# Retention weight sums: signs turned, and most of the sums made by transfers that add to their target

## The chip, the cores and the metric

The kernel runs on one core of one Trainium2 chip. The metric is the device time of one execution in microseconds (us). TensorE (PE) does the matrix products, VectorE (DVE) and ScalarE (ACT) the elementwise work, SyncE (SP) issues most transfers, and GpSimd (POOL) issues a few.

## What is computed

Two layers over 512 latent and 256 context tokens of width 1024: windowed attention with a SwiGLU FFN, then bidirectional retention with a SwiGLU FFN. The change lies in the second layer's token mixer. Cut to what matters:

```
q_x, k_x, v_x, g_x = split(h_x @ w_qkvg)      # 4 heads: q, k 256 wide, v, g 512 wide
k_c, v_c           = split(h_c @ w_qkvg[...]) # context: keys and values only
ox_f = retention_chunked(q_x, k_x, v_x, log_g[0], state_f)         # forward
ox_b = retention_chunked(flip(q_x), flip(k_x), flip(v_x), ...)     # backward
y    = normalise(ox_f + flip(ox_b)) * gn_gain
out  = (silu(g_x) * y) @ w_o
```

## The kernel before, in words

All products are float32 in three passes: each operand t is split into a high part hi = round(t) by a cast on ACT (L164) and a low part lo = t - hi by a subtraction on DVE (L165), and a product is hi·hi + lo·hi + hi·lo. So each weight chunk of 128 x 1024 float32 (512 KB in HBM, array `wst`) is loaded, cast and subtracted before TensorE reads it.

**The quarter scheme.** For the latent tokens the product of the activations with [k q] (and with [v g]) of one head is done on 2 x 2 blocks with seven quarter products in place of eight (a Winograd form of Strassen's scheme). The activations' quarter sums are made once, in `token_sums` (L1225). The weights' quarter sums are made for each of the four heads, from raw chunks, before they are split. With the block names of the code, before the change:

- k and q (one chunk a block): q12 := q22 - q12 (L1411); r11 := q12 + k11 (L1412); r21 := k21 - r11 (L1415); r11 := q22 - r11 (L1416).
- v and g (two chunks a block, i = 0, 1): g12 := g22 - g12 (L1449); v11 := g12 + v11 (L1450); v21 - v11 (L1456; in head 0 by L1465 and L1466 instead: ACT negates v11, then a transfer issued by POOL adds v21 to it); g12 - v11 (L1537), from raw chunks that are loaded a second time.

Each of these is one DVE instruction on 128 x 1024 elements, apart from head 0's L1465 and L1466.

**The order of a head.** Program order in the loop at L1362: k products and context keys; the k and q sums, their splits and products (`product_q`, L1274), which leave in q and k (tiles `qt`, `kt`) by copies (L1425, L1428, L1437) and by additions (L1431, L1434); rotary positions of q (`rope_pair`, L1296); for heads 1 to 3 the other value products (`other_values`); the v and g sums with the splits w2 (of v11 after L1450), w3 (of g12) and w4 (of the v21 sum); rotary positions of k; the value products 2, 3 and "22" (`product_v`, L1285), with copies out of the two banks `Yv` by ACT: L1478 after product 2, L1481 after product 3, L1487 after "22". Tile 0 of "22" (`last_values(0)`), the first scores, and then tile 1 of "22" (`last_values(1)`) follow. Six rounds of scores and accumulation follow (L1495 to L1531). Then come the splits w1 of the fourth sum (L1537) and w22 of g22, the gate products 1 and 4, which are added to `gate` (L1544, L1597), normalisation, gating, and the output projection (L1609 to L1622).

**Buffers.** Raw chunks go to the ring `wraw` (two buffers) or, where `chunk(i, True)` asks for it, to `wx` (four buffers, which the scores also use). Split weights go to four pairs `whi`/`wlo` that rotate: the split that comes four later waits until TensorE has done with its pair. `chunk` issues on SP (L1204), which takes its transfers one after another and stands still while the next one's buffer is in use.

**Order on the engines.** Every engine executes its own instructions strictly in order. That order is fixed when the kernel is compiled, by a list scheduler with a model of how long instructions and transfers take. It takes, of what its model holds to be ready, what comes first in the program. So L1537, which stands behind the scores in the program, executes ahead of and between them. `after(ins, others)` (L91) puts an instruction behind others on its engine.

Of the kernel before, what the change touches and what calls it, by code (L numbers as in the profile page):

```python
# [11 lines left out]
AF = mybir.ActivationFunctionType  # L12
# [18 lines left out]
HALVES = (slice(0, 256), slice(256, 512))  # L31
# [18 lines left out]
def dit_kernel(ctx, tc, xT, cT, crow, small, consts, masks, tabs0, tabs1, jtab, adaQ, adaN, adaT, wst, out):  # L50
    nc = tc.nc
    mult, add, sub = ALU.mult, ALU.add, ALU.subtract
# [9 lines left out]
    def T(pool, cols, tag, bufs, dt=F32):  # L62
        return pool.tile([P, cols], dt, tag=tag, bufs=bufs, name=tag)

    def pj(n=512):
        return T(psJ, 512, "pj", 2)[:, :n]
# [24 lines left out]
    def after(ins, others):  # L91
        for o in others:
            tc.add_manual_dep(ins.ins, o.ins.name, order, reason="table set turn")
# [32 lines left out]
    def w_parts(pool, own=2):  # L126

        bufs = own
        if ring:
            pool, bufs = ring[wsel[0] % len(ring)], 2  # L130
        elif wsel[0] % (2 + own) < 2:
            pool, bufs = rp, 2
        wsel[0] += 1
        return T(pool, 1024, "whi", bufs, F32R), T(pool, 1024, "wlo", bufs, F32R)
# [28 lines left out]
    def split(t, hi, lo, behind=()):  # L163
        after(nc.scalar.copy(hi, t), behind)  # L164
        return nc.vector.tensor_tensor(lo, t, hi, op=sub)  # L165
# [207 lines left out]
    raw = []  # L373
# [289 lines left out]
    for t in range(6):  # L663
        v = T(akv, 256, "v", 6)
# [134 lines left out]
    t1 = cp.tile([P, 8], F32, name="lg_t1")  # L799
    t2 = cp.tile([P, 8], F32, name="lg_t2")  # L800
# [68 lines left out]
    for d4 in range(0, KT, 4):  # L869
# [4 lines left out]
        for d in range(d4, d4 + 4):  # L874
            o = pj(SX)
# [75 lines left out]
    def token_sums():  # L951

        h1, h2 = THIRDS
        for k in range(4):
            t1, t2 = tm[k], tm[k + 4]
            for j in (k, k + 4):
                nc.scalar.activation(tm[j][:, h1], tm[j][:, h1], AF.Identity, bias=mods[0, 0][:, 3, j:j + 1])
            nc.vector.tensor_tensor(t2[:, h2], t1[:, h2], t2[:, h2], op=add)
            nc.vector.tensor_tensor(t1[:, h2], t1[:, h1], t1[:, h2], op=sub)
            nc.vector.tensor_tensor(t1[:, h1], t2[:, h2], t1[:, h1], op=sub)  # L960
            nc.vector.tensor_tensor(park[:, k * 384:(k + 1) * 384], t2[:, h1], t1[:, h1], op=sub)
            for n, t in ((1, t2[:, h2]), (3, t1[:, h2]), (2, t1[:, h1])):
                S[n, k] = parts(quarter())
                split(t, *S[n, k])
# [226 lines left out]
    qp = R.enter_context(tc.tile_pool(name="qp", bufs=1, reuse_waits="tile"))  # L1191
# [3 lines left out]
    h_sum = [(T(hS, 512, "sA", 16, F32R), T(hS, 512, "sA", 16, F32R)) for _ in range(KT)]  # L1195
# [6 lines left out]
    def chunk(i, own=False):  # L1202
        raw = T(qw, 1024, "wx", 4) if own else T(rp, 1024, "wraw", 2)
        nc.sync.dma_start(raw, wst[i])  # L1204
        return raw

    def split_chunk(raw, behind=()):
        w = w_parts(hpool[0])
        last_split[0] = split(raw, *w, behind)
        return w  # L1210

    last_split, rope_end, rope_sum, hm, other_sums = [None], [None], [None], [], []
# [9 lines left out]
            return lambda k: first(4 * (n[1] == "2") + k, int(n[0]) - 1)  # L1222
        return of

    def token_sums(hm, part, sh2, sums, behind=()):  # L1225

        q1, q2 = HALVES
        shift = mods[1, 0][:, part]
        nc.vector.tensor_tensor(sh2[:, 0:4], shift[:, 0:4], shift[:, 4:8], op=add)
        for k in range(4):  # L1230
            t1, t2 = hm[k], hm[k + 4]
            after(nc.vector.scalar_tensor_tensor(t2[:, q2], t1[:, q2], sh2[:, k:k + 1], t2[:, q2], add, add), behind)
            nc.vector.tensor_tensor(t1[:, q2], t1[:, q1], t1[:, q2], op=sub)
            nc.vector.scalar_tensor_tensor(t1[:, q1], t2[:, q2], shift[:, k:k + 1], t1[:, q1], sub, sub)
            mid = split(t1, *sums[2 * k + 1])
            nc.vector.scalar_tensor_tensor(t2[:, q1], t2[:, q1], shift[:, k + 4:k + 5], t1[:, q1], add, sub)
            other_sums.append((t2, *sums[2 * k]))
        return mid

    def other_parts():  # L1240
        while other_sums:
            split(*other_sums.pop(0))
# [21 lines left out]
    def context_norm(behind):  # L1264
        ssq[1] = t_y(1)
        neg_half_rstd(ssq[1], t_sq(SC), ctx_sum[0], D, behind)
        h, last = norm_mod(1, 1, 0, cres)
        h_ctx.extend(h)
        return last
# [4 lines left out]
    def product_q(o, a, w, first):  # L1274

        for k in range(4):
            xhi, xlo = a(k)
            for e in range(2):
                ws = slice(k * 256 + e * P, k * 256 + e * P + P)
                for i, (p, r) in enumerate(((w[0], xhi), (w[1], xhi), (w[0], xlo))):  # L1280
                    ins = nc.tensor.matmul(o[:, e * SC:(e + 1) * SC], p[:, ws], r, start=first and k + e + i == 0,  # L1281
                                           stop=k == 3 and i == 2, skip_group_check=True)
        return ins
# [77 lines left out]
    normed = context_norm([ins])  # L1361
    for hd in range(RH):  # L1362
        bq = chunk_base + 16 * hd
        bv, bg = bq + 4, bq + 8
# [16 lines left out]
        r11, r21 = chunk(bq), chunk(bq + 1)  # L1381
        k11, k21 = split_chunk(r11), split_chunk(r21)
        if hd == 0:
            sums = token_sums(hm, 0, T(qp, 16, "sh2", 1), h_sum, [normed])
            dx, dcx = strips(0, [sums])
        cos1, sin1 = rope_tables()
        Y, X, kc = W4("Y"), W4("X"), W4("X")
        kt, qt = [[T(qa, 512, "gate", 4) for _ in range(2)] for _ in range(2)]
# [19 lines left out]


        q12, q22 = chunk(bq + 2, True), chunk(bq + 3, True)  # L1410
        nc.vector.tensor_tensor(q12, q22, q12, op=sub)  # L1411
        nc.vector.tensor_tensor(r11, q12, r11, op=add)  # L1412
        w2 = split_chunk(r11, () if hd else [sums])
        other_parts()
        nc.vector.tensor_tensor(r21, r21, r11, op=sub)  # L1415
        nc.vector.tensor_tensor(r11, q22, r11, op=sub)  # L1416
        w1 = split_chunk(r11)
        first = [] if hd else [last_split[0]]
        for ins in later:
# [1 line left out]
        w3, w22, w4 = (split_chunk(r, first) for r in (q12, q22, r21))  # L1421
# [6 lines left out]
            nc.scalar.copy(qt[e][:, HALVES[1]], o)  # L1428
        product_q(Y, quarter_of(3), w3, False)
        for e, o in halves(Y):  # L1430
            nc.vector.tensor_tensor(qt[e][:, HALVES[1]], qt[e][:, HALVES[1]], o, op=add)  # L1431
        product_q(Y2, quarter_of(4), w22, False)
        for e, o in halves(Y2):
            nc.vector.tensor_tensor(qt[e][:, HALVES[0]], qt[e][:, HALVES[0]], o, op=add)  # L1434
        product_q(Y, quarter_of("22"), w4, False)
        for e, o in halves(Y):
            nc.scalar.copy(kt[e][:, HALVES[1]], o)  # L1437
# [5 lines left out]
        g12, w2, w4 = [], [], []  # L1443
        v11 = []
        for i in range(2):
            g12.append(chunk(bg + i, True))
            g22 = chunk(bg + 2 + i, True)
            v11.append(chunk(bv + i))
            nc.vector.tensor_tensor(g12[i], g22, g12[i], op=sub)  # L1449
            nc.vector.tensor_tensor(v11[i], g12[i], v11[i], op=add)  # L1450
            w2.append(split_chunk(v11[i]))
        if hd:
            w3 = [split_chunk(g) for g in g12]
            for i in range(2):
                v21 = chunk(bv + 2 + i, True)
                nc.vector.tensor_tensor(v21, v21, v11[i], op=sub)  # L1456
                w4.append(split_chunk(v21))
        else:

            ready, w3, lows = last_split[:], [], []  # L1460
            for g in g12:
                w3.append(split_chunk(g))
                lows += last_split
            for i in range(2):
                nc.scalar.activation(v11[i], v11[i], AF.Identity, scale=-1.0)  # L1465
                nc.gpsimd.dma_start(v11[i], wst[bv + 2 + i], accum_op=add)  # L1466
            qh = rope_pair(qt, cos1, sin1, ready)
            for low in lows:
                after(low, rope_sum)
# [5 lines left out]
        gate = [T(qa, 512, "gate", 4) for _ in range(4)]  # L1475
# [6 lines left out]
        if hd == 0:  # L1482
            w4 = [split_chunk(v, rope_end) for v in v11]
# [49 lines left out]

        w1 = []
        for i in range(2):
            g, v = chunk(bg + i), chunk(bv + i)
            after(nc.vector.tensor_tensor(g, g, v, op=sub), [] if hd else rope_end)  # L1537
            w1.append(split_chunk(g))
        w22 = [split_chunk(chunk(bg + 2 + i)) for i in range(2)]
        Zg = [W4("Z"), W4("Z")]  # L1540
        last = hd == RH - 1
        product_v(Zg, quarter_of(1), w1, True)
        for t in range(2):
            nc.vector.tensor_tensor(gate[2 + t], gate[2 + t], Zg[t], op=add)  # L1544
        product_v(Zg, quarter_of(4), w22, False, (0,))


# [21 lines left out]
        def gated(n):  # L1569
            silu(gate[n], gate[n])  # L1570
            nc.vector.tensor_tensor(gate[n], ov[n], gate[n], op=mult)
# [22 lines left out]
            turned(HALVES[1])  # L1594
        product_v(Zg, quarter_of(4), w22, False, (1,))
        for t in range(2):
            nc.vector.tensor_tensor(gate[t], gate[t], Zg[t], op=add)  # L1597
            gated(t)
        if not last:

# [23 lines left out]
        for i in range(4):  # L1624
            if i < 2:
                raw = w_raw()
# [20 lines left out]
        hm = [T(hM, 512, "hm", 8) for _ in range(KT)]  # L1647
# [45 lines left out]
    sh2 = T(fp, 48, "sh2", 1)  # L1693
# [263 lines left out]
```

## Time and profile before

| | |
|---|---|
| median of 3 runs | 1734.41 us (1733.25 to 1735.33) |
| profiled execution | 1732.25 us |
| its span in the trace | 1730.3 us |
| retention, 876 to 1366 us: TensorE busy | 485.51 of 490.00 us |
| the same: VectorE, ScalarE, GpSimd busy | 377.12, 233.11, 1.75 us |
| granted TensorE clock | 1.00 in the retention stretch, 0.999 over the span |

The span is the time from the first to the last instruction of the profiled execution; that execution took 1.95 us more in all, and was 2.16 us faster than the median. L1537 is line 1537 of the kernel. An instruction with the letter q behind its engine (SPq) is the sequencer's: it waits or issues. The four heads begin at about 876, 1000, 1123 and 1246 us.

### The profile page before, as it was taken

What the parts mean: (1) busy time and instruction counts of PE and PEld (TensorE: products, weight loads), DVE (VectorE), ACT (ScalarE), POOL (GpSimd) and SP (SyncE); (2) the same over time, 40 slices, a digit from 0 to 9 for tenths busy, and PEclk for the clock granted to TensorE, in tenths of its full rate; (3) what the DMA queues carried; (4) which work ended last, traced back from release to release, by engine and by line L of the source; (5) the groups of instructions that cost most, each with busy time, mean ns of one, the idle gap of its engine ahead of it and who ended that gap; (6) DMA issues with size and microseconds to landing.
All of it is one profiled execution on the core that took longest, in us unless ns stands there. A gap on an engine that the chain in (4) does not pass through costs nothing.

```text
span 1730.3 us, 27786 instructions
## 1 busy us (share of the span) xinstructions
PE 1698.0 (98%) x10876; PEld 1513.0 (87%) x10876; DVE 1361.0 (79%) x2436; ACT 871.1 (50%) x1552; POOL 50.5 (3%) x168
## 2 busy tenths in 40 slices
PE   7999999999999999999999999999999999999999
PEld 5788877899999999999988788898897899899998
DVE  6698889798778788787889858858758798877874
ACT  5587779465433334342556534524525464445442
POOL 0000000000000000000000000000000000000000
PEclk9999999999999999999999999999999999999999
DMA  9612221543253434343423524523423223333322
GB/s 349 239 30 57 62 62 56 209 134 121 73 157 117 153 110 148 123 154 102 156 99 88 183 77 132 163 82 124 159 90 108 95 74 103 117 102 116 100 86 86
DMA packets 62803, 207.48 MB, mean 120 GB/s; under 512 B 7248, under 2 KB 8912, under 8 KB 62416
## 3 DMA queue, kind: packets, MB, share of 16 engines
q1 hardware_dynamic: 55184, 178.97, 32.0%
q0 software_dynamic: 7200, 26.22, 5.2%
q8 instruction: 85, 1.39, 0.3%
q10 hardware_dynamic: 288, 0.52, 0.1%
q14 instruction: 46, 0.38, 0.1%
HBM read 199.65 MB, written 2.10 MB: 117 GB/s over the span
## 4 chain that ended last, share of the span: by engine, by line
PE 78%; DVE 11%; DMA 6%; ACT 3%; issue 2%; SPq 0%; ACTq 0%; DVEq 0%
PE Y L897 14%; PE pj L147 7%; PE Z L897 7%; PE pj L149 7%; PE pj L148 7%; PE Z L1292 6%; PE X L897 3%; DMA wraw<-in_wst_dram 3%; PE pT L736 2%; PE pO L750 2%; PE S L710 2%; DVE wlo L165 2%; PE Y L1281 2%; PE pj L1292 2%; PE X L1281 1%
## 5 line engine op out<-in xcount | busy, mean ns | idle before, releaser
L164 ACT CAST whi<-wraw 128x1024 fp32r<-128x1024 f32 x258 | 270.0, 1051 | 333.7 <-PE Z L149 81.9
L165 DVE TENSOR_TENSOR wlo<-wraw,whi 128x1024 fp32r<-128x1024 f32 x258 | 314.3, 1221 | 64.5 <-ACT whi L164 62.7
L897 PE MATMUL Y<-aq,whi 128*128 128x384 f32 x640 | 173.5, 335 | 0.6 <-ACT hn L1053 0.6
L897 PEld LDWEIGHTS Y<-aq,whi 128*128 128x128 f32 x640 | 116.6, 188 | 1.6 <-ACT hn L1053 1.4
L256 DVE SCALAR_TENSOR_TENSOR res<-pj,mod,res 128x512 f32<-128x512 f32 (+1 forms) x112 | 81.0, 728 | 41.5 <-PE pj L149 41.2
L897 PE MATMUL Y<-aq,wlo 128*128 128x384 f32 x320 | 107.0, 334 | 0.0
L273 DVE CUSTOM_DVE_ANT_0 y<-adaw,crow,small_sb 128x1024 bf16<-128x1024 f32 x64 | 81.9, 1280 | 29.6 <-DMA adaw<-in_adaT_dram 29.4
L1292 PE MATMUL Z<-whi,sA 128*128 128x512 f32 x256 | 81.7, 394 | 1.4 <-ACT gate L1478 1.4
L101 ACT ACTIVATE pr<-pr,stat,qs 128x513 f32<-128x513 f32 (+2 forms) x96 | 74.2, 775 | 9.1 <-DVE stat L717 8.8
L147 PE MATMUL pj<-ax,whi 128*128 128x512 f32 x176 | 69.0, 392 | 1.2 <-DVE res L256 1.2
L149 PE MATMUL pj<-ax,whi 128*128 128x512 f32 x176 | 68.6, 390 | 0.0
L148 PE MATMUL pj<-ax,wlo 128*128 128x512 f32 x176 | 68.6, 390 | 0.0
L147 PE MATMUL pj<-act,whi 128*128 128x512 f32 x168 | 65.6, 391 | 0.0
L148 PE MATMUL pj<-act,wlo 128*128 128x512 f32 x168 | 65.5, 390 | 0.0
L149 PE MATMUL pj<-act,whi 128*128 128x512 f32 x168 | 65.5, 391 | 0.0
L897 PEld LDWEIGHTS Y<-aq,wlo 128*128 128x128 f32 x320 | 60.1, 188 | 0.0
L1292 PEld LDWEIGHTS Z<-whi,sA 128*128 128x128 f32 x256 | 48.0, 188 | 13.0 <-ACT gate L1478 2.6
L711 DVE CUSTOM_DVE_ANT_0 pr<-S,mask,qs 128x256 f32<-128x256 f32 (+1 forms) x96 | 53.1, 566 | 7.8 <-PE S L710 5.3
L897 PE MATMUL Y<-sA,whi 128*128 128x256 f32 x304 | 58.1, 277 | 0.6 <-ACT res L1746 0.6
L897 PE MATMUL Y<-hx,whi 128*128 128x256 f32 x304 | 56.3, 277 | 0.0
L736 PE MATMUL pT<-const_sb,pr 128*128 128x128 f32 x352 | 53.6, 278 | 1.5 <-ACT tt L738 0.9
L1292 PE MATMUL Z<-wlo,sA 128*128 128x512 f32 x128 | 50.7, 396 | 0.2
(581 smaller groups left out, 5070.4 us busy)
## 6 DMA issues: line engine op xcount, KB each, us to landing
wraw<-in_wst_dram SPq DMA_DIRECT2D x224, 512.0 KB, 3.6
adaw<-in_adaT_dram POOLq DMA_DIRECT2D x48, 512.0 KB, 3.9
wx<-in_wst_dram SPq DMA_DIRECT2D x30, 512.0 KB, 4.3
adan<-in_adaQ_dram SPq DMA_DIRECT2D x16, 512.0 KB, 8.8
adan<-in_adaN_dram SPq DMA_DIRECT2D x12, 512.0 KB, 7.7
adaw<-in_adaT_dram SPq DMA_DIRECT2D x8, 512.0 KB, 3.9
res<-in_xT_dram SPq DMA_DIRECT2D x14, 256.0 KB, 3.2
aq<-in_adaN_dram SPq DMA_DIRECT2D x12, 256.0 KB, 5.7
```

Of the source, the lines that this page charges most:

```text
L101: ins = nc.scalar.activation(*args, **kw)
L147: nc.tensor.matmul(o, whi, xhi, start=first, stop=False)
L148: nc.tensor.matmul(o, wlo, xhi, start=False, stop=False)
L149: return nc.tensor.matmul(o, whi, xlo, start=False, stop=last)
L164: after(nc.scalar.copy(hi, t), behind)
L165: return nc.vector.tensor_tensor(lo, t, hi, op=sub)
L256: return nc.vector.scalar_tensor_tensor(res[d], o, mods[l, s][:, part, d:d + 1], res[d], mult, add)
L273: res.append(nc.vector.tensor_tensor_reduce(junk, w, cr[:, s * 1024:(s + 1) * 1024], 1.0, sm_t[:, C_ADAB + l * 48 + j:C_ADAB + l * 48 + j ...
L711: nc.vector.tensor_tensor_reduce(pt[:, c0:c0 + w], bank, mask[:, m0:m0 + w], 1.0, top, add, ALU.min, lo)
L736: nc.tensor.transpose(tp[:, a * P:(a + 1) * P], self.pr[(0, 2, 1, 3)[a]][:, ki * P:(ki + 1) * P], ident)
L897: nc.tensor.matmul(o, p, r, start=first and k + i == 0, stop=k == 3 and i == 2, skip_group_check=not first)
L1292: ins = nc.tensor.matmul(os[t], p, r, start=first and k + i == 0, stop=k == 3 and i == 2, skip_group_check=by_k or not first)
```

## The change

It turns the signs so that the sums are plain additions: q12 + q22, g12 + g22, v11 + v21 and g12 + v11 take the place of the differences. The difference of signs is taken up in the activations' quarter sums (two operators of `token_sums` turned for this layer) and in four places where product banks are added to `qt` and `gate`, which become subtractions of the same shape. The four sums named are then no longer made by DVE: a transfer issued by POOL reads the second operand from HBM and adds it to the first, which an earlier transfer has put into SBUF. Head 0's negation on ACT goes. r21 := k21 + r11, r11 := r11 - q22, r11 := q12 + k11 and v11 := g12 + v11 stay on DVE.

The raw chunks g22 (first load), v21 and the second v11 are no longer loaded to a buffer of their own. v11 stays in its `wraw` buffer until v21 has been added and the sum has been split (as in head 0 before). In head 0, L1537 stood behind the rotary work (`rope_end`); nothing takes the place of that order for w1.

```diff
+    def add_chunk(raw, i):
+        nc.gpsimd.dma_start(raw, wst[i], accum_op=add)
...
-    def token_sums(hm, part, sh2, sums, behind=()):
+    def token_sums(hm, part, sh2, sums, behind=(), ops=(add, sub)):
...
-        nc.vector.tensor_tensor(sh2[:, 0:4], shift[:, 0:4], shift[:, 4:8], op=add)
+        plus, minus = ops
+        nc.vector.tensor_tensor(sh2[:, 0:4], shift[:, 0:4], shift[:, 4:8], op=plus)
...
-            after(nc.vector.scalar_tensor_tensor(t2[:, q2], t1[:, q2], sh2[:, k:k + 1], t2[:, q2], add, add), behind)
+            after(nc.vector.scalar_tensor_tensor(t2[:, q2], t1[:, q2], sh2[:, k:k + 1], t2[:, q2], add, plus), behind)
...
-            nc.vector.scalar_tensor_tensor(t2[:, q1], t2[:, q1], shift[:, k + 4:k + 5], t1[:, q1], add, sub)
+            nc.vector.scalar_tensor_tensor(t2[:, q1], t2[:, q1], shift[:, k + 4:k + 5], t1[:, q1], add, minus)
...
-            sums = token_sums(hm, 0, T(qp, 16, "sh2", 1), h_sum, [normed])
+            sums = token_sums(hm, 0, T(qp, 16, "sh2", 1), h_sum, [normed], (sub, add))
...
         q12, q22 = chunk(bq + 2, True), chunk(bq + 3, True)
-        nc.vector.tensor_tensor(q12, q22, q12, op=sub)
+        add_chunk(q12, bq + 3)
         nc.vector.tensor_tensor(r11, q12, r11, op=add)
         w2 = split_chunk(r11, () if hd else [sums])
         other_parts()
-        nc.vector.tensor_tensor(r21, r21, r11, op=sub)
-        nc.vector.tensor_tensor(r11, q22, r11, op=sub)
+        nc.vector.tensor_tensor(r21, r21, r11, op=add)
+        nc.vector.tensor_tensor(r11, r11, q22, op=sub)
...
-            nc.vector.tensor_tensor(qt[e][:, HALVES[1]], qt[e][:, HALVES[1]], o, op=add)
+            nc.vector.tensor_tensor(qt[e][:, HALVES[1]], qt[e][:, HALVES[1]], o, op=sub)
...
-            nc.vector.tensor_tensor(qt[e][:, HALVES[0]], qt[e][:, HALVES[0]], o, op=add)
+            nc.vector.tensor_tensor(qt[e][:, HALVES[0]], o, qt[e][:, HALVES[0]], op=sub)
...
             g12.append(chunk(bg + i, True))
-            g22 = chunk(bg + 2 + i, True)
+            add_chunk(g12[i], bg + 2 + i)
             v11.append(chunk(bv + i))
-            nc.vector.tensor_tensor(g12[i], g22, g12[i], op=sub)
             nc.vector.tensor_tensor(v11[i], g12[i], v11[i], op=add)
             w2.append(split_chunk(v11[i]))
         if hd:
             w3 = [split_chunk(g) for g in g12]
             for i in range(2):
-                v21 = chunk(bv + 2 + i, True)
-                nc.vector.tensor_tensor(v21, v21, v11[i], op=sub)
-                w4.append(split_chunk(v21))
+                add_chunk(v11[i], bv + 2 + i)
+                w4.append(split_chunk(v11[i]))
         else:
...
             for i in range(2):
-                nc.scalar.activation(v11[i], v11[i], AF.Identity, scale=-1.0)
-                nc.gpsimd.dma_start(v11[i], wst[bv + 2 + i], accum_op=add)
+                add_chunk(v11[i], bv + 2 + i)
...
-            g, v = chunk(bg + i), chunk(bv + i)
-            after(nc.vector.tensor_tensor(g, g, v, op=sub), [] if hd else rope_end)
+            g = chunk(bg + i)
+            add_chunk(g, bv + i)
             w1.append(split_chunk(g))
...
-            nc.vector.tensor_tensor(gate[2 + t], gate[2 + t], Zg[t], op=add)
+            nc.vector.tensor_tensor(gate[2 + t], Zg[t], gate[2 + t], op=sub)
...
-            nc.vector.tensor_tensor(gate[t], gate[t], Zg[t], op=add)
+            nc.vector.tensor_tensor(gate[t], Zg[t], gate[t], op=sub)
```

## The prediction, made before the changed kernel ran

> **What bounds the kernel now.** I read the page's busy shares first, then the windows of the four heads, then what TensorE, DVE and SP waited for there.
>
> ```profile
> PE 1698.0 (98%) x10876; PEld 1513.0 (87%) x10876; DVE 1361.0 (79%) x2436; ACT 871.1 (50%) x1552; POOL 50.5 (3%) x168
> ```
> ```profile
> 876.00:1000.00 124.00, 120.83 (x666) 102.91 (x664) 111.23 (x180) 74.57 (x125) 1.75 (x2) 1.00 0.44 136
> 1000.00:1123.00 123.00, 122.89 (x653) 104.69 (x652) 90.18 (x122) 54.62 (x81) 0.00 (x0) 1.00 0.38 119
> 1123.00:1246.00 123.00, 122.81 (x653) 104.69 (x652) 90.03 (x121) 54.51 (x81) 0.00 (x0) 1.00 0.38 121
> sum 490.00, PE 485.51 PEld 413.36 DVE 377.12 ACT 233.11 POOL 1.75; mean PE 121.38 PEld 103.34 DVE 94.28 ACT 58.28 POOL 0.44
> ```
> ```profile
> PE Z L1292 <- ACT gate L1478: 1.4, 1, 1.4
> PE Y L1281 <- DVE wlo L165: 0.8, 1, 0.8
> PE X L1519 <- ACT wx L164: 0.5, 1, 0.5
> PE pj L147 <- ACT qk L1587: 0.5, 1, 0.5
> PE X L1582 <- DVE gate L1571: 0.5, 1, 0.5
> PE Z L1292 <- DVE wlo L165: 0.4, 1, 0.4
> ```
>
> The second fence has, after the stretch, the busy time of PE, weight loads, DVE, ACT and POOL, then the granted clock, the DMA share and GB/s; its last row sums the four heads. TensorE bounds the stretch: 485.51 of 490.00 us busy. DVE, which the change relieves, is busy 111.23 of 124 us in head 0, where TensorE has 3.2 us idle, and about 90 of 123 in heads 1 and 2, where TensorE has 0.11 and 0.19 us idle. So **no relief of DVE can bring more than 4.5 us**. The third fence splits 4.1 us of that; the waits on L1587 and L1571 (1.0 us) are the last head's end, which the change doesn't touch. **3.5 us** are left as the most that can be won, nearly all in head 0.
>
> **What goes from DVE and ACT.** Rows of DVE's groups, then single lines:
>
> ```profile
> L1537 DVE TENSOR_TENSOR wraw<-wraw 128x1024 f32<-128x1024 f32 x8 | 9.8, 1221 | 8.4 <-DMA wraw<-in_wst_dram 8.4
> L1449 DVE TENSOR_TENSOR wx<-wx 128x1024 f32<-128x1024 f32 x8 | 9.8, 1219 | 2.1 <-DMA wx<-in_wst_dram 2.1
> L1456 DVE TENSOR_TENSOR wx<-wx,wraw 128x1024 f32<-128x1024 f32 x6 | 7.1, 1214 | 0.0
> ```
> ```profile
> L1411 DVE TENSOR_TENSOR wx<-wx x4: 1215/1216/1219, 891.1 to 1238.9; 128x1024 f32<-128x1024 f32 x4
> ```
> ```profile
> L1412 DVE TENSOR_TENSOR wraw<-wx,wraw x4: 1209/1224/1225, 915.5 to 1258.1; 128x1024 f32<-128x1024 f32 x4
> ```
> ```profile
> 925.71 0.33 SPq L1204 DMA_DIRECT2D wx<-in_wst_dram  x1
> 927.98 0.33 SPq L1204 DMA_DIRECT2D wraw<-in_wst_dram  x1
> ```
> ```profile
> 930.02 1.22 DVE L1449 TENSOR_TENSOR wx<-wx 128x1024 f32<-128x1024 f32 x1 [0.93 <-DMA wx<-in_wst_dram]
> ...
> 932.96 1.22 DVE L1450 TENSOR_TENSOR wraw<-wx,wraw 128x1024 f32<-128x1024 f32 x1
> ```
> ```profile
> DMA to landing us min/median/max: 3.4/3.7/7.8
> ```
>
> The last row is of the loads that `chunk` issues (L1204). DVE loses 8 + 8 + 6 + 4 = 26 instructions of 1.22 us, 31.7 us in all; ACT loses head 0's two negations. This counts only where TensorE waits. In head 0, L1449 for i = 1 waits for a g22 that SP could issue only at 925.71, since the `wx` buffers were full. Without g22 in `wx` the two q and two g chunks fill its four buffers at the head's start, and L1450 waits only for v11: issued 927.98, plus 3.7, is 931.7, against 932.96. The rotary chain and the copy L1478 behind it come 1.3 us earlier, so 1.3 of the 1.4 us go. The 0.5 us on `wx` lies behind the splits of the late w22 chunks, which come earlier; I take it whole. The 0.8 us (L1281) stands behind L1412 and L1416, which stay. **Gain 1.8 us**; ends 0 and 3.5. Where a sign turns, operation and shape stay: L1411 (a subtraction) 1216 ns, L1412 (an addition) 1224. Cost nothing.
>
> **What the transfers cost.** Only head 0 has had such additions, two of them:
>
> ```profile
> L1466 POOL DMA_DIRECT2D wraw<-in_wst_dram x2: 861/872/884, 934.4 to 939.0; - x2
> ...
> DMA to landing us min/median/max: 5.3/5.7/6.1
> ```
> ```profile
> 934.00:946.00 12.00, 10.64 (x52) 8.61 (x52) 11.49 (x19) 6.99 (x12) 1.75 (x2) 1.00 0.54 87
> 1028.00:1033.00 5.00, 5.00 (x47) 5.00 (x46) 0.97 (x3) 0.65 (x2) 0.00 (x0) 1.00 0.34 105
> 980.00:1000.00 20.00, 20.00 (x98) 16.68 (x96) 18.31 (x31) 12.29 (x18) 0.00 (x0) 1.00 0.61 208
> ```
>
> An addition holds POOL 0.87 us and lands 5.7 us after issue, 4.5 us later than a 1.22 us DVE sum that starts with it; and it starts only when its target has landed. On the DMA engines the two took 0.54 x 12 / 2 = 3.2 us each (nothing else was issued there); one plain load took 0.34 x 5 = 1.7 us. Heads 1 to 3 get seven additions for six loads: 22.4 - 10.2 = 12.2 us of 123, so the share rises from 0.38 to 0.48. POOL gets 6.1 us in a head where it now has 0.00, and issues in the order in which targets land; SP issues six fewer.
>
> *q12 and g12: nothing.* L1411 runs at 891.1 and 1238.9, L1412 after it at 915.5 and 1258.1: the sum lies 24 and 19 us ahead of its reader, cover for 4.5 us. Without it L1412, the split w2 and TensorE would be late by the difference.
>
> *v21: nothing in heads 1 to 3, with little to spare.* Head 1, ACT, then DVE:
>
> ```profile
> 1065.84 1.05 ACT L164 CAST whi<-wx 128x1024 fp32r<-128x1024 f32 x1 [0.63 <-PE Z L1292]
> 1068.18 1.04 ACT L164 CAST whi<-wx 128x1024 fp32r<-128x1024 f32 x1
> ```
> ```profile
> 1060.59 1.21 DVE L1456 TENSOR_TENSOR wx<-wx,wraw 128x1024 f32<-128x1024 f32 x1
> 1061.72 1.21 DVE L165 TENSOR_TENSOR wlo<-wraw,whi 128x1024 fp32r<-128x1024 f32 x1
> ```
>
> The first two are the casts of w4: their `whi` pair is TensorE's until then. The addition to v11[1] can be issued after w2's last subtraction, which ends at 62.93 and moves up by some 1.2 us without L1456; plus 5.7 is 1067.4, ahead of 68.18. Head 0's w4 stands behind the rotary work anyway.
>
> *w1: this costs.* Before, its chunk loads hung only on L1456. Now v11 keeps its `wraw` buffer until w4 is split, and two transfers come in series.
>
> ```profile
> 1073.52 1.06 ACT L164 CAST whi<-wraw 128x1024 fp32r<-128x1024 f32 x1 [1.17 <-DVE wraw L1537]
> 1074.48 0.58 ACT L1481 COPY gate<-Z 128x512 f32<-128x512 f32 x1
> ```
> ```profile
> 1076.73 0.39 PE L1292 MATMUL Z<-whi,aq 128*128 128x512 f32 x1
> ```
> ```profile
> 1079.60 1.22 DVE L1537 TENSOR_TENSOR wraw<-wraw 128x1024 f32<-128x1024 f32 x1 [1.98 <-DMA wraw<-in_wst_dram]
> ```
> ```profile
> 1202.89 1.23 DVE L1537 TENSOR_TENSOR wraw<-wraw 128x1024 f32<-128x1024 f32 x1 [2.00 <-DMA wraw<-in_wst_dram]
> ```
>
> The first cast of w1 (73.52) stands on ACT ahead of the copy L1481, which frees the bank that TensorE needs at 76.73. And the compiled order believes in fast transfers: twice here DVE stands 2 us before L1537 for a chunk that has not landed. With two transfers in series that error grows, and the cast will stand as early as now. Sum: w4[0] cast 1065.84 + 1.05, its subtraction 1.22 = 1068.1; load 3.7 = 1071.8; addition 5.7 = 1077.5; cast 1.06 = 1078.6; copy 0.58 = 1079.2. TensorE is held 2.4 us; **7.3 us in heads 1 to 3**. Behind the cast on ACT also stand L1487 and the scores' casts; on DVE the cast's subtraction stands before the first scores' multiplication. If L1481 comes first, these are what is held, so much the same time is at stake. Ends: nothing (the cast placed after all that TensorE waits for), and 4.1 us a head (subtraction as late as it is now, landing at 6.1 and some sharing), 12.3 in all; I take the sum from the medians. In head 0 two rounds of scores are ready before w1's cast; nothing there.
>
> **Sum.** -1.8 + 7.3 = +5.5 us. The profiled execution took 1732.25 us (span 1730.3, and 1.95 around it), 2.16 under the median; so 1737.8 for it and **1739.9** for a median like that shown.
>
> **Rivals.** *The additions stay hidden* (ends faster): the cast of w1 stands behind L1481 and the first scores' cast, or the addition lands 2.5 us sooner than my sum (1075.0 instead of 1077.5), from which point nothing is held. Then the gain stands alone: 1734.41 - 1.8 = 1732.6, at best 1730.9. For it: TensorE needs w1 itself only at the end of the scores. Against: the rows of L1537. The Trainium skill's "DMA: Bandwidth & Descriptors", section "Anatomy of one DMA — SWDGE (gpsimd) path", gives a transfer that GpSimd issues 2.0 us plus its bytes at 436 GB/s, by my estimate 3.2 us for 512 KB; by that rule w1 would land at 1075.0 and this rival would hold. The trace's 5.3 to 6.1 us for the adding transfers speaks against it.
>
> *Transfers get in each other's way*, on top of the forecast. After a head's scores the DMA share is 0.61 already (980 to 1000); three additions for one load bring 0.61 x 20 + 9.6 - 1.7 = 20.1 us of work into 20.
>
> ```profile
> 992.29 1.06 ACT L164 CAST whi<-wraw 128x1024 fp32r<-128x1024 f32 x1 [1.05 <-DMA wraw<-in_wst_dram]
> 993.25 0.63 ACT L107 ACTIVATE gate<-gate 128x512 f32<-128x512 f32 x1
> ```
> ```profile
> 996.65 0.38 PE L1582 MATMUL X<-const_sb,gate 128*128 128x128 f32 x2
> ```
>
> A weight load behind one addition lands 3.2 us later and holds ACT, with the gate's activation behind it; that ends at 993.9 and has some 2 us before the transposes at 996.65. 1.2 us in each of heads 0 to 2: 1743.5.
>
> *Nothing moves*: other waits take what DVE gives back, and w1 is hidden: 1734.4.
>
> **Chances.** Forecast 0.48 (its own range 1735 to 1743), hidden 0.30, contention 0.12, nothing 0.10. A measurement of this kernel tells about 0.2%, 3.5 us, from no change, so the bounds are 1730.9 and 1737.9. Faster: 0.14 of the hidden case (a little more relief than I count) and 0.01 of the forecast: 0.15. Same: 0.16 + 0.10 + 0.12 of the forecast: 0.38. Slower: 0.35 + 0.12 = 0.47. The range 1731.5 to 1744.5 leaves out the better half of the hidden case's spread and the tail of contention.
>
> **What would show it.** Right: in heads 1 to 3 ACT or DVE stands some 4 us before w1's cast for a transfer, and TensorE waits 2 to 3 us for L1481 or for a cast of the scores; head 0's wait on L1478 is under 0.3 us; L1466's kind lands 5 to 6 us after issue. Wrong: TensorE idle stays under 0.3 us in heads 1 to 3, or w4's casts wait for their addition, or the casts of w1 come after the first scores.

## The result, and the profile after

The kernel after took 1746.72 us (median of 6 runs, 1744.82 to 1750.77) against 1734.20 us for the kernel before beside it (6 runs): **slower by 12.5 us**, ratio 1.0072 with a 95% interval of 1.0061 to 1.0083. The forecast was 1739.9 us, and the range ended at 1744.5. The profiled execution of after took 1750.77 us, with a span of 1748.6 us, so it is the slowest of the six. Line numbers of after lie 1 to 4 above those of before from L1285 on: the scores' matmuls are L1507 to L1509, their accumulation L1520 to L1522, the first scores' multiplication L1512, and the new transfers L1208.

The page's busy line and TensorE's waits in the retention stretch, 876 to 1380 us (waiting instruction, what it waited for, total us, times, longest):

```profile
PE 1708.5 (98%) x10876; PEld 1520.8 (87%) x10876; DVE 1333.2 (76%) x2410; ACT 868.9 (50%) x1550; POOL 72.7 (4%) x194
```
```profile
PE X L1520 <- ACT wx L164: 9.1, 4, 2.8
PE X L1522 <- DVE wx L165: 1.8, 3, 0.6
PE Z L1296 <- DVE wlo L165: 1.1, 2, 0.7
```

DVE is busy 27.8 us less, as meant (31.7 were forecast). Head 0's wait for the copy of `gate` has gone from the list. In its place stands one wait in each of the four heads, for a cast of the scores. TensorE's busy time *rose* by 10.5 us although it executes the same 10876 matmuls; that is a second loss, shown further down.

The timeline of head 1 in after shows where the wait comes from (start, duration, engine, line, in brackets the idle time before it and what ended it):

```profile
1075.39 0.87 POOL L1208 DMA_DIRECT2D wraw<-in_wst_dram  x1 [10.27 <-DMA wraw<-in_wst_dram]
1075.59 0.59 ACT L1482 COPY gate<-Z 128x512 f32<-128x512 f32 x1 [2.16 <-PE Z L1296]
...
1078.08 0.86 POOL L1208 DMA_DIRECT2D wraw<-in_wst_dram  x1 [1.81 <-DMA wraw<-in_wst_dram]
...
1082.22 1.05 ACT L164 CAST whi<-wraw 128x1024 fp32r<-128x1024 f32 x1 [6.04 <-DMA wraw<-in_wst_dram]
...
1083.30 1.23 DVE L165 TENSOR_TENSOR wlo<-wraw,whi 128x1024 fp32r<-128x1024 f32 x1 [10.49 <-ACT whi L164]
1083.39 0.39 PE L1509 MATMUL pj<-qk 128*128 128x512 f32 x1
1084.44 0.68 DVE L1512 SCALAR_TENSOR_TENSOR hn<-pj,dx 128x512 f32<-128x512 f32 x1
...
1084.93 1.04 ACT L164 CAST whi<-wraw 128x1024 fp32r<-128x1024 f32 x1 [1.18 <-DMA wraw<-in_wst_dram]
1085.88 0.61 ACT L164 CAST wx<-hn 128x512 fp32r<-128x512 f32 x1
...
1086.54 0.79 PE L1520 MATMUL X<-wx 128*128 128x512 f32 x1 [2.76 <-ACT wx L164]
```

The two additions of w1 are issued at 1075.39 and 1078.08 and land 6.7 and 6.8 us later. ACT stands 6.04 us before w1's first cast for the first of them. DVE stands 10.49 us before that cast's subtraction, and the first scores' multiplication (L1512) is behind it. ACT stands another 1.18 us for the second addition, and the cast of the first scores (1085.88) is behind that. TensorE, which needs this cast, issues its last matmul at 1083.39 and its next at 1086.54.

**The second loss is the clock.** Stretches of after around that pause (stretch, length, then busy us of PE, weight loads, DVE, ACT and POOL; the third number from the end is the granted clock):

```profile
1078.00:1083.70 5.70, 5.70 (x26) 4.41 (x24) 0.40 (x1) 1.48 (x2) 0.86 (x1) 1.00 0.93 165
1086.50:1089.90 3.40, 3.24 (x7) 2.13 (x8) 3.12 (x5) 2.56 (x4) 0.00 (x0) 0.50 0.69 237
1089.90:1093.30 3.40, 3.40 (x11) 2.64 (x10) 2.50 (x4) 1.67 (x2) 0.00 (x0) 0.56 0.55 159
1093.30:1098.00 4.70, 4.70 (x22) 3.90 (x21) 2.43 (x4) 1.24 (x2) 0.00 (x0) 1.00 0.42 124
...
1215.80:1219.20 3.40, 3.40 (x8) 2.73 (x9) 2.71 (x4) 1.70 (x3) 0.00 (x0) 0.50 0.53 166
...
1342.10:1345.50 3.40, 2.94 (x7) 2.39 (x8) 3.34 (x5) 1.73 (x3) 0.00 (x0) 0.50 0.52 154
...
966.50:969.90 3.40, 2.79 (x7) 2.15 (x7) 3.40 (x6) 1.93 (x3) 0.00 (x0) 0.52 0.55 154
969.90:973.30 3.40, 3.40 (x9) 2.64 (x8) 2.12 (x3) 2.28 (x3) 0.00 (x0) 0.50 0.53 154
```

Before the pause the clock is 1.00, behind it 0.50 to 0.56 for 6.8 us, then 1.00 again. Heads 2 and 3 have 3.4 us of it, head 0 has 6.8. The account of the profiled execution: pauses of 2.19, 2.93, 2.52 and 2.15 us (from the distances of the matmuls' starts, less the usual 0.23) make 9.8 us, and six stretches of 3.4 us at half clock lose 10.2 us, 20.0 together. That agrees with the starts of the same matmuls in before: around the scores the four heads fall back by 5.0, 5.6, 4.6 and 3.9 us, 19.1 in all. Ahead of the scores head 0 gains 2.0 us and heads 1 to 3 gain 1.4, so the retention stretch loses 15.6 us of the 18.3 by which the spans differ. Of the rest, 0.2 us come before this stretch and 2.5 behind it; the record shows no cause for these. The six runs of after differ along with their clock: two with a mean clock of 0.992 took 1750.6 and 1750.8 us, four with 0.994 took 1744.8 to 1746.8. The only trace is of the slowest of them; which falls of the clock the faster four lack is not on record.

### The profile page after: what moved, and what is told of

Its sections match the earlier page's. It is cut to its first block, busy times and chain, and to the rows that moved or that the text cites. A ratio compares the mean times of both kernels' runs of the same rounds, so it can differ in the third digit from the quotient of the medians.

```text
span 1748.6 us, 27807 instructions
## 1 busy us (share of the span) xinstructions
PE 1708.5 (98%) x10876; PEld 1520.8 (87%) x10876; DVE 1333.2 (76%) x2410; ACT 868.9 (50%) x1550; POOL 72.7 (4%) x194
## 4 chain that ended last, share of the span: by engine, by line
PE 77%; DVE 10%; DMA 8%; ACT 3%; issue 2%; SPq 0%; ACTq 0%; POOLq 0%; DVEq 0%
PE Y L897 13%; PE pj L147 7%; PE pj L149 7%; PE pj L148 7%; PE Z L897 6%; DMA wraw<-in_wst_dram 4%; PE Z L1296 4%; PE X L897 3%; PE Y L1285 3%; PE pT L736 2%; DVE wlo L165 2%; PE pj L1296 2%; PE pO L750 2%; PE S L710 2%; PE X L1285 2%
## 5 line engine op out<-in xcount | busy, mean ns | idle before, releaser
L164 ACT CAST whi<-wraw 128x1024 fp32r<-128x1024 f32 x264 | 276.3, 1050 | 346.2 <-PE Z L149 80.2
L165 DVE TENSOR_TENSOR wlo<-wraw,whi 128x1024 fp32r<-128x1024 f32 x264 | 321.8, 1222 | 114.4 <-ACT whi L164 113.3
L1296 PE MATMUL Z<-whi,sA 128*128 128x512 f32 x256 | 80.9, 392 | 0.0
L1296 PEld LDWEIGHTS Z<-whi,sA 128*128 128x128 f32 x256 | 48.0, 188 | 10.3
L1296 PE MATMUL Z<-wlo,sA 128*128 128x512 f32 x128 | 50.4, 394 | 0.7 <-DVE wlo L165 0.7
```

Source lines behind the costliest of these rows:

```text
L1296: ins = nc.tensor.matmul(os[t], p, r, start=first and k + i == 0, stop=k == 3 and i == 2, skip_group_check=by_k or not first)
```

## The experiments

The theory, called W: ACT and DVE stand in their fixed order for w1's late additions, the scores' casts behind them hold TensorE, and each pause also costs clock. The rivals: L, the load that the adding transfers put on the DMA engines; H, which keeps W's pause but lays w1's lateness on v21's addition, which keeps the buffers that w1's loads need; and that the clock does not matter. Every time below is compared with runs of the kernel before on the same chip; the ratio is given with its 95% interval.

| kernel | median us | before beside it | ratio |
|---|---|---|---|
| after | 1746.72 | 1734.20 | 1.0072 (1.0061 to 1.0083) |
| v21_w1_by_dve | 1730.32 | 1734.96 | 0.9974 (0.9963 to 0.9985) |
| only_w1 | 1734.05 | 1734.96 | 0.9996 (0.9987 to 1.0006) |
| w1_by_dve | 1732.75 | 1734.84 | 0.9988 (0.9979 to 0.9998) |
| w1_in_wx | 1736.91 | 1734.25 | 1.0014 (1.0004 to 1.0024) |
| filled_idle | 1740.26 | 1734.96 | 1.0032 (1.0019 to 1.0046) |
| w1_behind_2 | 1739.25 | 1734.96 | 1.0024 (1.0010 to 1.0037) |
| w1_2_out_behind | 1727.51 | 1734.25 | 0.9964 (0.9953 to 0.9976) |
| v21_w1_dve_out_behind | 1729.04 | 1734.25 | 0.9971 (0.9960 to 0.9981) |
| before_out_behind | 1735.39 | 1734.84 | 1.0003 (0.9993 to 1.0012) |
| head0_only | 1732.32 | 1734.25 | 0.9990 (0.9981 to 1.0000) |

### Which sums cost: v21 and w1 given back to DVE

```diff
-                add_chunk(v11[i], bv + 2 + i)
-                w4.append(split_chunk(v11[i]))
+                v21 = chunk(bv + 2 + i, True)
+                nc.vector.tensor_tensor(v21, v21, v11[i], op=add)
+                w4.append(split_chunk(v21))
...
-            g = chunk(bg + i)
-            add_chunk(g, bv + i)
+            g, v = chunk(bg + i), chunk(bv + i)
+            after(nc.vector.tensor_tensor(g, g, v, op=add), [] if hd else rope_end)
```

> The sum of w1 in all heads and that of v21 in heads 1 to 3 are DVE's again, with loads of their own; q12's and g12's sums stay transfers that add. Theory W (ACT stands in its fixed order before w1's cast for a late addition, the scores' cast behind it holds TensorE, and TensorE's clock falls after each such pause): all pauses go and the gain of head 0 stays, 1732.6 us, 1731 to 1735. Rival L (the load that adding transfers put on the DMA engines, whichever sum they make): 12 of the 26 additions stay, so some half of the loss stays, 1738 to 1742.

Measured 1730.32 us, faster than before by 4.6 and 0.7 below W's range. All four pauses ahead of the scores are gone; so W's account of them holds, and the load of the other additions is not the loss. One long pause is new, 2.95 us at head 0's transposes, with 3.4 us at half clock behind it. TensorE's wait and, below it, ACT at that place:

```profile
PE X L1584 <- DVE gate L1573: 3.2, 2, 2.8
```
```profile
993.90 1.04 ACT L164 CAST whi<-wraw 128x1024 fp32r<-128x1024 f32 x1 [5.61 <-DMA wraw<-in_wst_dram]
994.85 0.63 ACT L107 ACTIVATE gate<-gate 128x512 f32<-128x512 f32 x1
```

The cast belongs to the output projection's weights. ACT stands 5.61 us for their load, and the last gate activation stands behind it.

### w1's sum alone by transfer

Here q12, g12 and, in heads 1 to 3, v21 are DVE's sums with loads of their own, and w1 stays as in after.

```diff
-        add_chunk(q12, bq + 3)
+        nc.vector.tensor_tensor(q12, q22, q12, op=add)
...
+            g22 = chunk(bg + 2 + i, True)
-            add_chunk(g12[i], bg + 2 + i)
+            nc.vector.tensor_tensor(g12[i], g22, g12[i], op=add)
...
-                add_chunk(v11[i], bv + 2 + i)
-                w4.append(split_chunk(v11[i]))
+                v21 = chunk(bv + 2 + i, True)
+                nc.vector.tensor_tensor(v21, v21, v11[i], op=add)
+                w4.append(split_chunk(v21))
```

> Only w1's sum is a transfer that adds; q12, g12 and v21 in heads 1 to 3 are DVE sums with loads of their own, as before. Theory W without a part for v21: w1's additions pause TensorE in all four heads, and head 0's gain is missing: 1734 plus 14 to 18, 1748 to 1752 us. Rival H (w1 is late because v21's addition keeps v11 in the wraw buffers that w1's loads need; w1's addition alone would be early enough): pauses in head 0 alone, where v21 was added by a transfer before too: 1734 plus 5, 1738 to 1741. Rival L: 8 additions more than before, 1736 to 1740, with no pause at a place of its own.

Measured 1734.05 us, the same as before: better than any theory had it. POOL, then ACT, in head 1 of this kernel:

```profile
1068.60 0.86 POOL L1208 DMA_DIRECT2D wraw<-in_wst_dram  x1 [108.50 <-ACT wx L164]
1070.86 0.85 POOL L1208 DMA_DIRECT2D wraw<-in_wst_dram  x1 [1.40 <-DVE hn L1305]
```
```profile
1078.71 1.05 ACT L164 CAST whi<-wraw 128x1024 fp32r<-128x1024 f32 x1 [1.27 <-DMA wraw<-in_wst_dram]
...
1081.66 0.62 ACT L164 CAST wx<-hn 128x512 fp32r<-128x512 f32 x1 [1.41 <-DVE hn L1514]
```

w1's additions start at 1068.60 and 1070.86, 6.8 and 7.2 us earlier than in after, since v11 leaves its `wraw` buffer early. Both of w1's casts stand ahead of the scores' cast here too, and yet that one (1081.66) waits only for its own scores. So **in heads 1 to 3 the addition to w1 alone costs nothing**. In head 0, where v21 was added by a transfer before the change too, TensorE pauses: 1.3 us and, two matmuls later, 0.8 us, and one stretch of lowered clock follows. That is some 3 us in place of H's 5, and heads 1 to 3 give it back: the 1860 matmuls whose starts I compare below take 346.8 us in this kernel, 348.6 in before.

### v21's sum alone by transfer, w1's by DVE

The diff is the lower half of the first one.

> The kernel after with w1's sum alone given back to DVE, with loads of its own; v21, q12 and g12 stay transfers. Theory H (v21's addition keeps both wraw buffers, and w1's four loads must go through them one pair after the other): w1 is still late in heads 1 to 3, TensorE pauses 1 to 1.5 us ahead of the second scores, too short for the clock: 1733 to 1737 us. Rival (w1's own addition is all that is late): no pause there, 1729 to 1731, as with v21 on DVE as well.

Measured 1732.75 us. TensorE waits 1.8 us in all (three times, 0.6 at most) ahead of the second scores, about half of what H had; the time lies 0.25 us below its range and above the rival's. So v21's addition alone costs little. Only **both in series** make w1 late enough for a long pause, as after has them in every head and only_w1 in head 0.

### The same transfers, with w1's loads in other buffers

`w1_chunks(own)` is w1's loop of loads, additions and splits, with `chunk(bg + i, own)`:

```diff
+        if hd:
+            w1 = w1_chunks(True)
         pend = scores(0)
...
+        if hd == 0:
+            w1 = w1_chunks(False)
```

> The kernel after, with w1's chunks of heads 1 to 3 in the wx buffers, which come free ahead of v11's wraw, so that they are loaded and added to without waiting for v21; all sums stay transfers, and w1's casts stand as early on ACT as before. Theory H (the hold of v11's buffers makes w1 late): no pause ahead of the scores in heads 1 to 3, head 0's stays; pauses at the transposes as in w1_behind_2 may come: 1732 to 1739. Rival (w1's addition is too slow at that place in any buffer): 1744 to 1749.

Measured 1736.91 us, 9.8 below after. The pauses ahead of the scores in heads 1 to 3 are gone, though every sum is still a transfer: H again. (The edit also moves w1's loop ahead of the scores in the program, so that its transfers are issued earlier; no run separates the place from the buffers.) Shorter waits came ahead of that place, for subtractions of weights and for the copy that frees a bank of `gate`:

```profile
PE Z L1296 <- DVE wlo L165: 3.3, 5, 0.8
PE Z L1296 <- ACT gate L1479: 3.1, 3, 1.1
```

What holds these two was not followed further.

### The idle time filled with matmuls

```diff
         for m in range(1, 6):
             cur = scores(m)
+            if hd and m == 1:
+                for _ in range(8):
+                    nc.tensor.matmul(ov[0], kh[0][0][:, 0:P], qh[0][0], start=True, stop=True)
             accumulate(m - 1, *pend)
```

> The kernel after, with eight extra matmuls of 512 columns (1.8 us at full clock, their sums are overwritten) in heads 1 to 3 at the place where TensorE pauses, so that it stands only 0.3 to 1.1 us there. Theory C (about half of the loss, some 2 us a pause, is the clock that falls to half after a pause): the clock stays up in these heads, 1740 us, 1737 to 1742, though more is computed. Rival (the pause alone is the loss, or the clock falls for another reason): 1746 to 1749.

Measured 1740.26 us: 24 matmuls more, and 6.5 us less than after. TensorE's wait, and stretches behind the place of the pause in heads 1, 2 and 3:

```profile
PE X L1520 <- ACT wx L164: 3.5, 4, 1.4
```
```profile
1086.40:1089.80 3.40, 3.40 (x17) 2.81 (x16) 2.71 (x4) 1.53 (x2) 0.00 (x0) 1.00 0.62 164
1207.80:1211.20 3.40, 2.76 (x11) 1.98 (x12) 3.40 (x5) 2.65 (x4) 0.00 (x0) 1.00 0.54 171
1334.30:1337.70 3.40, 2.79 (x11) 2.02 (x12) 3.40 (x5) 2.59 (x4) 0.00 (x0) 1.00 0.58 171
```

The clock is 1.00 in all three. These matmuls bring the scores no earlier, so it is the idle time that lowers the clock. How much the clock costs is read from the half-clock stretches of after (10.2 us), not from this median: head 0, where nothing was added, had a pause of 0.8 us and no fall in this execution and so lost 4.3 us less than in after's profile. Around their scores heads 1 to 3 fall back by 10.2 us against before, where after has 14.1; those 3.9 us are what the added matmuls brought, their own time included.

### w1's casts put behind the third round's scores

```diff
-            split(sd, ss[:, 0:512], ss[:, 512:])
+            sc_end.append(split(sd, ss[:, 0:512], ss[:, 512:]))
...
-            w1.append(split_chunk(g))
+            w1.append(split_chunk(g, [sc_end[2]]))
```

> All transfers as in the kernel after; w1's two casts are put behind the cast of the third round's scores in ACT's order, so that the first two rounds no longer stand behind them. Theory W: the additions have landed by then, no pause, clock near 1.00, 1732.6 us, 1731 to 1735. Rival L: the same transfers at the same places, 1744 to 1748.

Measured 1739.25 us: neither. The pauses ahead of the scores are gone, and three others stand at the transposes of heads 0 to 2. TensorE's wait, then ACT, SP and the clock at the end of head 1:

```profile
PE X L1584 <- DVE gate L1573: 6.2, 3, 2.5
```
```profile
1113.45 0.63 ACT L107 ACTIVATE gate<-gate 128x512 f32<-128x512 f32 x1 [1.29 <-DVE gate L1599]
1119.67 1.04 ACT L164 CAST whi<-wraw 128x1024 fp32r<-128x1024 f32 x1 [5.58 <-DMA wraw<-in_wst_dram]
1120.62 0.62 ACT L107 ACTIVATE gate<-gate 128x512 f32<-128x512 f32 x1
```
```profile
1111.65 10.68 SPq L122 DMA_DIRECT2D wraw<-in_wst_dram  x3
```
```profile
1119.00:1122.60 3.60, 1.13 (x6) 0.65 (x4) 1.83 (x2) 2.90 (x4) 0.00 (x0) 1.00 0.70 198
1122.60:1126.00 3.40, 3.37 (x16) 3.37 (x17) 1.23 (x1) 2.55 (x4) 0.00 (x0) 0.51 0.48 154
```

A weight load issued at 1111.65, among three additions of the next head's sums, lets its cast begin only at 1119.67, 8 us later, and the last gate activation stands behind it. (Plain loads can crowd each other as well: of five that SP issued in before from 976.60 to 980.74, the last took 7.8 us.) This is the prediction's contention rival at the very place it named, larger than its 1.2 us. In after it does not show: there the casts behind the late load came after the activations.

### And the projection's casts put behind the last gate activation

```diff
-                w.append(next_w(hpool[0]))
+                w.append(next_w(hpool[0], behind=turn["silu"][-1:]))
```

> The kernel w1_behind_2 (all transfers of the kernel after; w1's casts behind those of the third scores) with one more change of order: the casts of the output projection's weights in heads 0 to 2 stand on ACT behind the last gate activation. In w1_behind_2 TensorE paused 1.5, 2.7 and 2.6 us at the transposes, behind a gate activation that stood behind such a cast, whose plain load had landed 8 us after issue among three additions. Theory Q (a late transfer costs only through what stands behind it in a queue): these pauses and the clock behind them go, 1728 to 1731 us. Rival S (the load is late for TensorE itself, which then waits for the projection's weights): 1735 to 1739.

Measured 1727.51 us, below the interval's lower end by 0.5: ratio 0.9964 (0.9953 to 0.9976). **This version beats both kernels, and it makes all the transfers of after.** The profile is of its slowest run, 1731.49 us. TensorE's longest waits in the retention stretch, and ACT at the end of head 1:

```profile
PE pj L147 <- ACT qk L1589: 1.0, 2, 0.6
PE Z L1296 <- DVE wlo L165: 0.8, 2, 0.4
PE X L1521 <- ACT wx L164: 0.6, 1, 0.6
```
```profile
1116.27 0.63 ACT L107 ACTIVATE gate<-gate 128x512 f32<-128x512 f32 x1 [1.70 <-DVE gate L1599]
...
1122.71 1.05 ACT L164 CAST whi<-wraw 128x1024 fp32r<-128x1024 f32 x1 [2.07 <-DMA wraw<-in_wst_dram]
```

ACT still stands 2.07 us for a weight load, with nothing behind it that TensorE needs soon. Theory Q holds: a late transfer costs through what is queued behind it.

### Controls of that order, and of the gain

> The kernel v21_w1_by_dve (1730.3 us; its one long pause, 2.9 us, stood at head 0's transposes behind the same cast) with the casts of the output projection's weights behind the last gate activation. Theory Q: 2.9 us and 1.7 of clock go, 1725 to 1728. Rival S: the wait moves to the projection, 1729 to 1731.

Its edit is the one line above, on v21_w1_by_dve. Measured 1729.04 us (0.9971), in S's interval. But TensorE's wait has not moved: its longest wait for a line in heads 0 to 3 is 0.7 us, and the pause at head 0's transposes is gone. The median is 1.3 us under v21_w1_by_dve's, on another chip, and the intervals overlap; the spans of the profiled executions differ by 1.9 us (1729.2 and 1727.3). So Q's 4.6 us were too much, and how much was won is not settled.

The same line changed in the kernel before:

> The kernel before, changed only in that the casts of the output projection's weights in heads 0 to 2 stand on ACT behind the last gate activation. Theory Q (that order pays only where transfers make the load late; before has no pause at the transposes): 1733 to 1735.5 us, no change. Rival (the order alone is the gain of the two fastest kernels): 1728 to 1731.

Measured 1735.39 us, ratio 1.0003: the order alone brings nothing. The gain of the two fastest kernels needs the transfers.

v21 and w1 as in v21_w1_by_dve, and q12's and g12's transfers kept in head 0 alone:

```diff
+        if hd:
+            nc.vector.tensor_tensor(q12, q22, q12, op=add)
+        else:
             add_chunk(q12, bq + 3)
```

(g12 in the same way.)

> q12 and g12 are added by transfers in head 0 alone; in heads 1 to 3 they, v21 and w1 are DVE sums, as before. Theory G (all the gain is head 0's start, where g22 no longer waits for a buffer, and additions elsewhere bring nothing): no pause at head 0's transposes, since head 1's additions are gone there, 1726 to 1729 us. Rival (the relief of DVE in heads 1 to 3 carries part of the gain): 1730 to 1733.

Measured 1732.32 us, in the rival's interval: theory G falls. Head 0's start brings about 2 us, of which 0.7 to 1.0 is left after that head in the profiles of the two fast kernels. Heads 1 to 3, where the prediction saw next to nothing to win, bring 3.3 us in v21_w1_dve_out_behind and 3.5 in w1_2_out_behind, by the starts of the same matmuls in before. (That makes 4.2 to 4.3 us in the retention stretch; the rest of the 5 to 7 us between the medians stands in no trace.) A stretch of before in head 1 shows where it comes from:

```profile
1080.84 0.39 PE L1519 MATMUL X<-wx 128*128 128x512 f32 x1
1081.06 0.39 PE L1520 MATMUL X<-wx 128*128 128x512 f32 x1
1081.48 0.50 PE L1521 MATMUL X<-wx 128*128 128x512 f32 x1
1081.82 0.40 PE L1519 MATMUL X<-wx 128*128 128x512 f32 x1
```
```profile
1080.75 0.68 DVE L165 TENSOR_TENSOR wx<-hn,wx 128x512 fp32r<-128x512 f32 x1
```

A matmul row lasts 0.39 us, but the next usually starts 0.23 us after it. L1521 (1081.48) starts 0.42 us after L1520, when DVE's subtraction has ended (1080.75 + 0.68 = 1081.43), and the one after it 0.34 us later. That is 0.3 us lost, of which the busy column shows next to nothing, since the rows still touch or nearly. Over the same 1860 matmuls of heads 1 to 3 before has 24 such distances of 0.3 to 0.6 us, 8.8 us in all, 3.3 more than 24 usual ones; v21_w1_dve_out_behind and w1_2_out_behind have four each, and the latter one of 0.8 us. That DVE's relief removes them fits what goes and stays, but no run changed DVE's load alone.

## Why the prediction was wrong

**What bounds the kernel.** Right for the kind, wrong for the way to the bound. "No relief of DVE can bring more than 4.5 us", "nearly all in head 0", was read from the busy column. Short waits do not show in it, as the rows above show, and heads 1 to 3 gave 3.3 and 3.5 us to the two fast kernels. w1_2_out_behind is 6.2 us faster by its ratio (0.0036 x 1734, with 4.2 as the lower end), its retention stretch 4.2 us shorter in the profile; that 4.5 us is passed is likely, not shown.

**The gain.** The size was right, 2.0 us against 1.8, but in part by luck. The wait on L1478 went, as forecast. The 0.8 us on L1281, which the prediction took to stay, went too: it is gone in every kernel that adds q12 by a transfer in head 0, and still there in only_w1 (at 924.4 us), where q12 is DVE's sum. A new wait of 0.7 us for a weight's subtraction (L1296, at 940.8 us) took most of that back, and some 0.4 us of shorter waits went besides. The 0.5 us on `wx` lie where the new pause is.

**q12 and g12: nothing; v21: nothing.** Right in after as a cost: w4's casts (1068.76 and 1070.41 us in head 1) wait for no addition, and TensorE waits for no sum of q or g. But v21's addition is one of the two in series that make w1 late.

**w1.** The mechanism was right: ACT stood 6 us and DVE 10 us for the addition, in order, ahead of the scores. The branch was the second one that it named: L1481 (L1482 in after) came first at 1075.59, and the scores' casts were held. What failed is the size, in three places. *"In head 0 two rounds of scores are ready before w1's cast; nothing there"* failed. ACT in head 0 of after:

```profile
960.43 1.05 ACT L164 CAST whi<-wraw 128x1024 fp32r<-128x1024 f32 x1 [4.11 <-DMA wraw<-in_wst_dram]
961.38 0.62 ACT L164 CAST wx<-res 128x512 fp32r<-128x512 f32 x1
964.26 1.04 ACT L164 CAST whi<-wraw 128x1024 fp32r<-128x1024 f32 x1 [2.27 <-DMA wraw<-in_wst_dram]
965.21 0.61 ACT L164 CAST wx<-hn 128x512 fp32r<-128x512 f32 x1
```

The first two rounds passed, but the third stood behind w1's second cast, and the sum had followed the first cast alone. There the sum had nothing, and head 0 lost 5.0 us. *The landing* was sized at 5.7 us, the median of additions that stood nearly alone; w1's two overlap and took 5.6 to 7.2 in the four heads. The pause itself still came out at the forecast's 2.4 us a head (2.9, 2.5, 2.2 in heads 1 to 3). *The clock* was not in the sum at all, and by the account above it is half of the loss (10.2 of 20.0 us). The Trainium skill's "TensorE: Matmul & The Clock Gate", section "Why this matters for your kernels", warns of idle gaps of more than about 3 us between bursts; by that rule none of these pauses, 2.93 us at most, would have lowered the clock, and the trace decides against it. The same page's section "What's actually happening" gives a window of about 3.4 us that runs freely; the stretches of 3.4 and 6.8 us at half clock agree with it, and so do the times at which they begin (last section).

**The rivals.** *Hidden* was wrong for after, but it is what the order decides: w1_2_out_behind has the additions hidden. *Contention* did not show in after; with w1's pauses gone it became the next one, 1.5 to 2.7 us a head and not 1.2. The estimate of 3.2 us that the prediction made from the Trainium skill's "DMA: Bandwidth & Descriptors", section "Anatomy of one DMA — SWDGE (gpsimd) path", fits no addition of after: they landed after 5.3 to 9.0 us.

**What would show it.** Each of its marks for "right" came true (ACT's stand, TensorE's 2 to 3 us for a cast of the scores, head 0's wait on the copy gone), except that the additions to `wx` and w1's landed later than 5 to 6 us. The marks could not tell the time, since the clock stood in none of them.

## What to carry to other kernels

Price a late transfer by what stands behind its reader in the engine's order, for every reader and every pass of the loop; the same transfers cost 12 us or gained 6 by the place of two groups of casts. In these traces a pause of TensorE of more than about 2 us counted about twice: its length, and 1.7 us for each 3.4 us at half clock behind it. And a busy column near 100% left out 3.3 us of short waits here; count the distances of matmul starts.

## What the runs showed of the hardware

**Where the clock falls.** In the retention stretch of these profiles each pause of 2.15 us or more (2.15, 2.19, 2.52 and 2.93 in after, 2.55 and 2.66 in w1_behind_2, 2.95 in v21_w1_by_dve) is followed by 3.4 or 6.8 us near half clock. Single pauses of 1.5 and 1.7 us (before at 942.6 us, w1_behind_2 at 997.9, only_w1 at 943.1) are followed by 1.00. Two pauses close together went either way: 1.3 and 0.8 us in only_w1 lowered the clock, 1.6 and 0.8 us in filled_idle did not. (In heads 0, 2 and 3 of after, too, a second pause of 0.8 us follows the first.)

So the length of one pause does not decide, but the traces show what goes with it. Within each trace the falls begin whole multiples of 3.413 us apart: 966.60, 1086.07, 1215.78 and 1342.07 in after are 35, 38 and 37 such windows from one to the next. I cut the retention stretch of all twelve profiles into these windows and added up in each what the distances of the matmuls' starts exceed the usual (0.23 us, 0.11 for the short ones). Eight windows at full clock have 2.13 to 2.96 us of such idle time, and the clock falls at the end of each. No other window at full clock has more than 2.01 us, and none is followed by a fall. So **in this stretch the clock fell after a fixed window of 3.4 us of which some 60% or more was idle**. The two pauses of only_w1 lie in one window (2.13 us), those of filled_idle in two (1.58 and 1.02). The windows lie differently in each trace (the fall that all twelve have ahead of the retention begins between 255.5 and 257.4 us), so a pause near 2 us may cost clock or not. Elsewhere this limit does not hold as it stands: at 17 us, among other matmuls, before has a window with 2.54 us that no fall follows, and at 254 us one with 1.97 us in w1_in_wx is followed by one.

**Additions by transfer.** Those into `wraw` landed 5.7 us after issue in the median, as the two before had; those into `wx` (q12 and g12, issued close together beside other loads) took 7.6. The queue's row of the page:

```profile
q0 software_dynamic: 10944, 39.85, 9.7%
```

Before it stood at 7200 packets, 26.22 MB and 5.2%. So 13.63 MB more cost 4.5% of 16 engines' span. In w1_behind_2 a plain load issued among three of them took 8 us, where the median in before is 3.7 and the longest 7.8.
